# The third branch's key and value rows in a slot of the weights' ring, and score products that go out four together

## The chip, the cores and the metric

The program runs on one core of one Trainium2 chip, as one launch. The metric is the device time of that launch in microseconds (us), lower is better. The kernel before took 898.96, 900.66 and 900.21 us in three runs, median 900.21 us. One more execution, which the profiler recorded, took 896.71 us; the instructions in its trace span 895.0 us of that, and every number from a trace below is of that execution.

A core has five engines that the text names: PE (matrix products and transposes), DVE, ACT and POOL (element-wise work), SP (here it only issues transfers). Each runs its own list of instructions in order and waits on semaphores for the others. ACT, POOL and SP also issue DMA transfers; an instruction that issues one stands in the engine's list like any other and can wait there. "PEld" is the part of PE that loads the stationary operand of a product.

## What is computed

One step of a decoder layer for a prompt of 512 rows and 8 single new rows ("samples"), width 1024, all in float32:

```
mod = silu(c) @ w_ada + b_ada
h = rmsnorm(x) * (1 + scale) + shift
u, q, k_c, v_c, k_s, v_s, k_w, v_w, g = split(h @ w_in)      # 512, 512, 6 x 128, 24 columns
o_ssm  = state space mixer(u), then a GLU
o_attn = sum over 3 branches of gate * attention             # compressed, selected, window
x = x + gate1 * (concat(norm(o_ssm), norm(o_attn)) @ w_out)
x = x + gate2 * (relu(h2 @ w_up) ** 2 @ w_down)
y = rmsnorm(x)
```

There are 8 query heads and 2 key/value heads (a group of 4 query heads shares one). The prompt attends to its own rows; each sample attends to 1024 past rows of a paged cache (selected branch) or to 512 rows of a window state. Outputs are y, the new key and value rows of the three branches and the new states.

## The kernel before

**Products.** A float32 product that must be exact is made of three: the operand is split into a high part and a rest (`split`: ACT writes the high part, DVE the rest), and hi*hi, hi*lo, lo*hi go to PE. Score products whose operand is plain float32 are one `matmul` call; in the trace such a call shows as two MATMUL rows.

**Order.** The code is written in stages, and a scheduler with a timing model puts the instructions of each engine in an order of its own, interleaving the stages. So a new dependency, or a tile in another place, moves rows on all engines. Pools of tiles give the waits: a tile of a tag with `bufs=n` takes the slot of the tile n before it, and its first write waits until that one has been read.

**Weights' ring.** `rawt` hands out tiles of 128 x 2048 from a ring of three slots. Loads of weights (`wada`, `wkv`, `wq`, `wglu`) and some gathers of cache rows (`rslc`) take turns in it, each load waits until the tile three places earlier has been used. The loads are issued by SP, in SP's order.

**Key and value projection** (`kv_proj(c)`, L640, for the branches c = 0, 1, 2). It loads 256 columns of `w_in` (`wkv`), splits them into two pairs wH, wL, and runs over five row tiles t: four of 128 prompt rows and one of 8 samples. Each makes 24 products into PSUM (`pkv`; two PSUM tiles, tag `pj`). For c = 1 and 2, ACT copies the keys into `kvt` (128 x 256, tag with 2 buffers; L669), the values into `Vx`, and issues two transfers to DRAM (L691, L692); PE transposes `kvt` (`pkt`), ACT and DVE split the transposes into `KH` and `KL`. For c = 2 ACT also reads the gates. A `kvt` of t = 2 takes the buffer of t = 0, so its copy waits until the transfer of t = 0 has landed.

**State space outputs** (`state_space_outputs(q)`, q = 0 to 3). For each q eight transfers bring `yc` (one buffer), four issued by SP and four by POOL; DVE reads it into `yf` (L905, L908), and a GELU follows on ACT and DVE. The `yc` of the next q waits for `yf` of this one.

**Query projection** (L915 to L929): two `wq` loads of 1 MB, four splits, 8 x 24 products (`pj`, L619); ACT and DVE write `QS`.

**Score products in fours.** `compressed_scores` (L1170) makes for each of two key heads a set of four products (`psc`, L1174), one for each query head, each into 32 of the 128 rows of one PSUM tile. `sample_keys` (L1030) does the same for four samples: it transposes four blocks of keys each (`pkT`, L1038), copies them out of PSUM to `ktS` (the first and third on ACT, the second and fourth on DVE), and makes a set of four products (`pS`, L1047), one for each sample, again into 32 rows each. It is called for two groups of samples of the window branch (one set each) and two of the selected branch (two sets each): six sets. With the two of `psc` there are eight sets, 32 products. Each product waits for its own operand alone, and the scheduler places each where it finds it ready.

**Around them** the prompt's softmax over 16 (branch, head) pairs runs (`softmaxed`: `pst`, `mxa`, `pe`; `values`: `ptp`, `PT`, `po`). In `values` a manual dependency is there already: the first of two products waits for the copy of the second one's operand (L1272).

Of the kernel before, what the change touches and what calls it, by code (L numbers as in the profile page):

```python
# [10 lines left out]
F32 = mybir.dt.float32  # L11
# [3 lines left out]
ALU = mybir.AluOpType  # L15
AX = mybir.AxisListType

P = 128
# [19 lines left out]
def body(tc, i, o, dbg=None):  # L38
    nc = tc.nc
# [11 lines left out]
    def banks(name, **tags):  # L51

        if "pool" in bank:
            bank["pool"].close()
        st = ExitStack()
        bank.update(pool=st, tile=st.enter_context(tc.tile_pool(name=name, bufs=1, space=PS, reuse_waits="tile")), tags=tags)
# [4 lines left out]
        return bank["tile"].tile([P, 512], F32, tag=tag, name=name, bufs=bank["tags"][tag])  # L61

    banks("pA", pj=2, ss=2, tr=2, ad=1, po=1)

    def split(h, l, src):
        nc.scalar.copy(h, src)  # L66
# [4 lines left out]
    def rawt(name):  # L71
        return raw.tile([P, 2048], F32, tag="raw", name=name)
# [560 lines left out]
            nc.sync.dma_start(uscr[q * P : (q + 1) * P, T:NT], uT[q][:, T:NT])  # L633

    onames = ("cmp", "slc", "win")

    def kv_proj(c):
        c0 = 1024 + 256 * c
        r = rawt("wkv").rearrange("p (k c) -> p k c", k=KT)
        nc.sync.dma_start(r, i["w_in"][0, :, c0 : c0 + 256].rearrange("(k p) c -> p k c", p=P))  # L640
        nw = 280 if c == 2 else 256
        if c == 2:
            rg = p1.tile([P, KT, 24], F32, name="rg")
            nc.sync.dma_start(rg, i["w_in"][0, :, 1792:1816].rearrange("(k p) c -> p k c", p=P))
        ws = []
        for kk in range(2):
            kr = slice(4 * kk, 4 * kk + 4)
            h, l = whl(4, nw)
            split(h[:, :, 0:256], l[:, :, 0:256], r[:, kr])
            if c == 2:  # L650
                split(h[:, :, 256:280], l[:, :, 256:280], rg[:, kr])
            ws.append((h, l))
        for t in range(5):
            tok = slice(t * P, t * P + (P if t < 4 else NB))
            mp = P if t < 4 else NB
            ps = pst("pj", "pkv")
            for k in range(KT):
                wh, wl = ws[k // 4]
                for n, (x, w) in enumerate(((hH, wh), (hH, wl), (hL, wh))):
                    nc.tensor.matmul(ps[0:mp, 0:nw], x[:, k, tok], w[:, k % 4], start=(k == 0 and n == 0),  # L660
                                     stop=(k == KT - 1 and n == 2))
            if t == 4:
                nc.scalar.copy(kvs[:, c * 256 : (c + 1) * 256], ps[0:NB, 0:256])
                if c < 2:
                    nc.scalar.dma_start(o["new_%s_sample" % onames[c]], kvs[:, c * 256 : (c + 1) * 256])
                else:
                    nc.scalar.dma_start(o["new_win_sample"][:, T - 1], kvs[:, 512:768])
            else:
                kvt = p1.tile([P, 256], F32, tag="kvt", name="kvt", bufs=2)  # L669
                out = o["new_%s_prompt" % onames[c]][tok]  # L670
                if c == 0:
                    nc.scalar.copy(kvt, ps[:, 0:256])
                    nc.scalar.dma_start(out, kvt)
                    pk = pst("tr", "pkc")
                    for n in range(2):
                        nc.tensor.transpose(pk[:, n * P : (n + 1) * P], kvt[:, n * P : (n + 1) * P], ident)
                    for g in range(2):
                        for j2 in range(2):
                            for n in range(2):
                                nc.vector.tensor_copy(  # L680
                                    xTp[j2 * 64 : j2 * 64 + 64, n, g, :, t * 8 : t * 8 + 8],
                                    pk[g * 64 : g * 64 + 64, n * P : (n + 1) * P].rearrange(
                                        "p (c jp j2) -> p j2 jp c", c=8, j2=2)[:, j2])
                else:
                    br = c - 1

                    kv2 = kvt.rearrange("p (g a d) -> p g a d", g=2, a=2)
                    nc.scalar.copy(kv2, ps[:, 0:P].rearrange("p (g d) -> p g d", g=2).unsqueeze(2).to_broadcast([P, 2, 2, HD]))
                    vt = Vx[:, t, 2 * br : 2 * br + 2]
                    nc.scalar.copy(vt, ps[:, P:256].rearrange("p (g d) -> p g d", g=2))  # L690
                    nc.scalar.dma_start(out[:, 0:P].rearrange("t (g d) -> t g d", g=2), kv2[:, :, 0])  # L691
                    nc.scalar.dma_start(out[:, P:256].rearrange("t (g d) -> t g d", g=2), vt)  # L692
                    pk = pst("tr", "pkt")
                    for g in range(2):
                        nc.tensor.transpose(pk[:, g * P : (g + 1) * P], kvt[:, g * P : (g + 1) * P], ident)
                    split(KH[:, 2 * br : 2 * br + 2, tok], KL[:, 2 * br : 2 * br + 2, tok],
                          pk[:, 0:256].rearrange("p (g t) -> p g t", g=2))
            if c == 2:
                sigmoid_(gates[0:mp, t], ps[0:mp, 256:280])
# [215 lines left out]
    for s in range(2):  # L915
        r = rawt("wq").rearrange("p (k c) -> p k c", k=KT)
        nc.sync.dma_start(r, i["w_in"][0, :, 512 + s * 256 : 512 + (s + 1) * 256].rearrange("(k p) c -> p k c", p=P))
        for m in range(2):
            wh, wl = wsplit(r[:, :, m * P : (m + 1) * P])
            h0 = 2 * (2 * s + m)  # L920
            for hf, ps in proj_half(wh, wl):
                ql = wp.tile([P, 520], F32, tag="mrow", name="ql")[0:64].rearrange("p (a b) -> p a b", a=2)
                w = min(HB, T - hf * HB)
                for hh in range(2):
                    pq_ = ps[hh * 64 : hh * 64 + 64]
                    qc = (h0 + hh, slice(hf * HB, hf * HB + w))
                    nc.scalar.activation(ql[:, hh], pq_, AF.Copy, scale=HD**-0.5)
                    nc.scalar.activation(QS[0:64, *qc], pq_[:, 0:w], AF.Copy, scale=HD**-0.5)
                    nc.vector.tensor_tensor(QS[64:128, *qc], ql[:, hh, 0:w], QS[0:64, *qc], ALU.subtract)  # L929
            nc.gpsimd.tensor_copy(qs[:, h0 : h0 + 2], ql[:, :, HB - NB : HB])  # L930
        state_space_outputs((2 + s,))
    dump("gates", gates)
# [96 lines left out]
    def sample_keys(br, grp, tiles, nj, gate):  # L1029
# [3 lines left out]
        for h in range(nj // 4):  # L1033
            kts = []
            for b4 in range(4):
                px = pst(("ad", "ss")[b4 % 2], "pkT")
                for j4 in range(4):
                    nc.tensor.transpose(px[:, j4 * P : (j4 + 1) * P], tiles[b4][:, 4 * h + j4, 0:P], ident)  # L1038
                kt = sb.tile([P, 512], F32, tag="ktS", name="ktS", bufs=4)
                if b4 % 2:  # L1040
                    nc.vector.tensor_copy(kt, px)
                else:
                    nc.scalar.copy(kt, px)
                kts.append(kt)
            S = pst("ss", "pS")
            for b4 in range(4):
                nc.tensor.matmul(S[b4 * 32 : b4 * 32 + 32], q4[:, 4 * grp + b4], kts[b4], start=True, stop=True)  # L1047
            if br == 0:
                nc.vector.tensor_tensor(t[:, h * 512 : (h + 1) * 512].rearrange("p (j k c) -> p j k c", j=4, c=8),
                                        S.rearrange("p (j k c) -> p j k c", j=4, c=8),  # L1050
                                        pens[grp].unsqueeze(1).unsqueeze(3).to_broadcast([P, 4, 16, 8]), ALU.add)
            else:
                nc.scalar.copy(t[:, 1:nk], S[:, 1:nk])
                nc.gpsimd.memset(t[:, 0:1], NEG)
# [115 lines left out]
    def compressed_scores():  # L1170
        for g in range(2):
            ps = pst("ss", "psc")
            for hh in range(4):
                nc.tensor.matmul(ps[hh * 32 : hh * 32 + 32], Kcp[:, g], QS[:, 4 * g + hh].bitcast(F32), start=True, stop=True)  # L1174
            nc.scalar.copy(etc[:, g], ps)

    held = {}
# [72 lines left out]
    def values(br, h0, pes, po):  # L1250

        kb = 2 * br + h0 // 4
        for part in (((0, 0),), ((1, 0), (3, 3 * P)), ((2, 0),)):
# [12 lines left out]
            for kt, c0 in part:  # L1266
                for hh, PT in enumerate(PTs):
                    mm = nc.tensor.matmul(po[hh * 64 : hh * 64 + 64, kt * P : T], Vx[:, kt, kb], PT[:, c0 : c0 + T - kt * P],  # L1268
                                          start=(br == 0 and kt == 0), stop=False)
                    if hh == 0:  # L1270

                        tc.add_manual_dep(mm.ins, turned_.ins.name, mybir.DependencyInfo(mybir.DependencyClass.Sync, mybir.DependencyReason.DATA))  # L1272

    glu_w = []
    mixs = {}
# [354 lines left out]
```

## Time and profile before

| what | us |
|---|---|
| median of three runs | 900.21 |
| profiled execution, whole | 896.71 |
| profiled execution, its instructions' span | 895.0 |
| of it PE busy | 845.8 |
| DVE busy | 519.8 |
| ACT busy | 389.9 |
| from 254 on: third branch's projection, to the first query product at 273.1 | about 19 |
| 305 to 442: prompt softmax and samples' attention, PE busy 131.58 of | 137 |
| 526 to the end: MLP | 369 |

A row of the timeline has the start, the duration, the engine, the line, the operation, what it writes and reads, how many, and in brackets how long the engine sat idle before it and what ended that. "ACTq", "SPq" are rows of instructions that issue a transfer. The chain is the work that ended last, followed back from the end of the program: a piece in it is time that the end waited for. Idle time of an engine off that chain costs nothing by itself.

### The profile page before, as it was taken

What the parts mean: (1) busy time and instruction counts of PE and PEld (TensorE: products, weight loads), DVE (VectorE), ACT (ScalarE), POOL (GpSimd) and SP (SyncE); (2) the same over time, 40 slices, a digit from 0 to 9 for tenths busy, and PEclk for the clock granted to TensorE, in tenths of its full rate; (3) what the DMA queues carried; (4) which work ended last, traced back from release to release, by engine and by line L of the source; (5) the groups of instructions that cost most, each with busy time, mean ns of one, the idle gap of its engine ahead of it and who ended that gap; (6) DMA issues with size and microseconds to landing.
All of it is one profiled execution on the core that took longest, in us unless ns stands there. A gap on an engine that the chain in (4) does not pass through costs nothing.

```text
span 895.0 us, 16400 instructions
## 1 busy us (share of the span) xinstructions
PE 845.8 (94%) x6527; PEld 751.8 (84%) x6527; DVE 519.8 (58%) x1365; ACT 389.9 (44%) x883; POOL 64.0 (7%) x147
## 2 busy tenths in 40 slices
PE   2799998999998999998989999999999999999996
PEld 1557997888987766756679989999999999999996
DVE  5876666785766466668667874442333444434533
ACT  1555317453435466556655554442111344433322
POOL 6001201000152100000000000000000000000000
PEclk9999998999999999999989999999999999999998
DMA  8957577473773441203266553333333333232302
GB/s 290 319 195 247 181 157 193 138 247 116 203 244 92 165 166 64 77 2 142 73 210 198 180 190 94 94 96 94 95 95 95 94 95 92 82 86 75 92 1 96
DMA packets 111836, 122.36 MB, mean 137 GB/s; under 512 B 24500, under 2 KB 91880, under 8 KB 109584
## 3 DMA queue, kind: packets, MB, share of 16 engines
q1 hardware_dynamic: 101968, 88.66, 32.8%
q0 software_dynamic: 5488, 29.99, 9.6%
q10 hardware_dynamic: 4304, 2.66, 1.1%
q8 instruction: 51, 0.84, 0.4%
q14 instruction: 25, 0.20, 0.1%
HBM read 112.47 MB, written 13.03 MB: 140 GB/s over the span
## 4 chain that ended last, share of the span: by engine, by line
PE 66%; DVE 2%; ACT 1%; issue 0%; ACTq 0%; DVEq 0%
PE pup L1427 21%; PE pdn L1427 21%; PE pwo L1427 5%; PE pj L619 3%; PE po L1268 2%; PE ptp L1261 2%; PE pg L1289 2%; PE pS L1047 2%; PE pst L1232 1%; PE pkT L1038 1%; PE pst L1233 1%; PE psc L1174 1%; PE pstat L879 1%; PE poS L1136 0%; PE po L1349 0%; PE pst L1234 0%
## 5 line engine op out<-in xcount | busy, mean ns | idle before, releaser
L1427 PE MATMUL pdn<-hidH,wL 128*128 128x256 f32 (+1 forms) x480 | 136.0, 283 | 0.0
L1427 PE MATMUL pdn<-hidL,wH 128*128 128x256 f32 (+1 forms) x480 | 135.8, 283 | 0.0
L1427 PE MATMUL pup<-h2L,wH 128*128 128x256 f32 (+1 forms) x480 | 135.5, 283 | 0.0
L1427 PE MATMUL pdn<-hidH,wH 128*128 128x256 f32 (+1 forms) x480 | 135.3, 282 | 0.0
L1427 PE MATMUL pup<-h2H,wL 128*128 128x256 f32 (+1 forms) x480 | 135.0, 282 | 0.0
L1427 PE MATMUL pup<-h2H,wH 128*128 128x256 f32 (+1 forms) x480 | 134.5, 283 | 0.0
L1427 PEld LDWEIGHTS pup<-h2L,wH 128*128 128x128 f32 x480 | 90.4, 188 | 0.8 <-DVE rs L105 0.8
L1427 PEld LDWEIGHTS pup<-h2H,wH 128*128 128x128 f32 x480 | 89.8, 188 | 0.8 <-ACT h2H L66 0.8
L1427 PEld LDWEIGHTS pdn<-hidH,wL 128*128 128x128 f32 x480 | 90.4, 188 | 0.0
L1427 PEld LDWEIGHTS pdn<-hidL,wH 128*128 128x128 f32 x480 | 90.2, 188 | 0.1
L1427 PEld LDWEIGHTS pup<-h2H,wL 128*128 128x128 f32 x480 | 90.3, 188 | 0.0
L1427 PEld LDWEIGHTS pdn<-hidH,wH 128*128 128x128 f32 x480 | 90.3, 188 | 0.0
L66 ACT CAST wH<-wdn 128x1024 fp32r<-128x1024 f32 x30 | 31.5, 1049 | 114.2 <-PE pdn L1427 104.3
L67 DVE TENSOR_TENSOR wL<-wup,wH 128x1024 fp32r<-128x1024 f32 x30 | 36.7, 1225 | 57.9 <-ACT wH L66 57.9
L67 DVE TENSOR_TENSOR wL<-wdn,wH 128x1024 fp32r<-128x1024 f32 x30 | 36.8, 1225 | 54.3 <-ACT wH L66 54.3
L401 PE MATMUL ph<-xc,w 128*128 128x256 f32 (+2 forms) x320 | 62.9, 346 | 0.7 <-DVE xc L391 0.7
L401 PEld LDWEIGHTS ph<-xc,w 128*128 128x128 f32 x320 | 50.8, 194 | 11.0 <-issue 5.4
L66 ACT CAST wH<-wup 128x1024 fp32r<-128x1024 f32 x30 | 31.5, 1050 | 47.3 <-PE pup L1427 37.5
L1507 ACT ACTIVATE rl<-pup 128x256 f32<-128x256 f32 (+1 forms) x64 | 24.5, 385 | 45.5 <-PE pup L1427 45.4
L389 ACT COPY xc<-pxc 64x256 f32<-64x256 f32 x96 | 32.1, 366 | 22.5 <-DVE xc L391 18.8
L1508 DVE TENSOR_TENSOR rl<-rl 128x256 f32<-128x256 f32 (+1 forms) x64 | 27.2, 426 | 22.9 <-ACT rl L1507 22.9
L1436 DVE SCALAR_TENSOR_TENSOR xT<-pdn,mod,xT 128x256 f32<-128x256 f32 x32 | 15.2, 478 | 41.7 <-PE pdn L1427 41.6
(569 smaller groups left out, 2038.8 us busy)
## 6 DMA issues: line engine op xcount, KB each, us to landing
wada<-w_ada SPq DMA_DIRECT2D x20, 1024.0 KB, 5.1
wup<-w_up SPq DMA_DIRECT2D x16, 1024.0 KB, 5.4
wdn<-w_down SPq DMA_DIRECT2D x16, 1024.0 KB, 5.7
wo<-w_out SPq DMA_DIRECT2D x8, 1024.0 KB, 5.5
wada<-w_ada SPq DMA_DIRECT2D x8, 512.0 KB, 16.0
rwin<-state_win SPq DMA_DIRECT2D x4, 1024.0 KB
new_win_sample<-state_win POOLq DMA_DIRECT2D x2, 2044.0 KB, 8.6
wkv<-w_in SPq DMA_DIRECT2D x3, 1024.0 KB, 8.1
```

Of the source, the lines that this page charges most:

```text
L66: nc.scalar.copy(h, src)
L67: nc.vector.tensor_tensor(l, src, h, ALU.subtract)
L389: nc.scalar.copy(dst[:, :, :, hf], srcv[:, :, :, hf])
L401: nc.tensor.matmul(phv[:, lo:hi, 0:w], w1[n][:, r_], xc[n][:, lo:hi, r_ % 8, off : off + w], start=(r_ == 0), stop=(r_ == 15))
L619: nc.tensor.matmul(ps[:, 0:HB], w[:, k], x[:, k, hc], start=(k == 0 and n == 0), stop=(k == KT - 1 and n == 2))
L1047: nc.tensor.matmul(S[b4 * 32 : b4 * 32 + 32], q4[:, 4 * grp + b4], kts[b4], start=True, stop=True)
L1261: nc.tensor.transpose(pt_[:, c : c + P], at(qt, kt * P, P), ident)
L1268: mm = nc.tensor.matmul(po[hh * 64 : hh * 64 + 64, kt * P : T], Vx[:, kt, kb], PT[:, c0 : c0 + T - kt * P], start=(br == 0 and kt == 0), s ...
L1289: nc.tensor.matmul(ps[:, 0:HB], r[:, k, c], zf[k][:, hc], start=(k == 0), stop=(k == 3))
L1427: nc.tensor.matmul(ps[:, 0 : b - a], w, x[:, a:b], start=first and n == 0, stop=last and n == 2)
L1507: nc.scalar.activation(rl, ps[:, 0 : b - a], AF.Relu)
L1508: nc.vector.tensor_tensor(rl, rl, rl, ALU.mult)
```

## The change

Three things. First, for c = 2 one tile of the weights' ring is taken behind `wkv` (`kvr`), and the keys of row tile t go to columns t*256 to t*256+255 of it, instead of to the two buffers of the tag `kvt`. Second, in `sample_keys` the first product of a set gets a dependency on the copies of the third and the fourth operand; third, in `compressed_scores` the first product of a set gets one on the last write of the fourth head's `QS`. The helper `not_before` makes such a dependency; `values` uses it in place of the same lines.

```diff
+    def not_before(mm, last):
+        tc.add_manual_dep(mm.ins, last.ins.name, mybir.DependencyInfo(mybir.DependencyClass.Sync, mybir.DependencyReason.DATA))
...
+    qlast = {}
...
+        kvr = rawt("kvt") if c == 2 else None
         for t in range(5):
...
-                kvt = p1.tile([P, 256], F32, tag="kvt", name="kvt", bufs=2)
+                kvt = kvr[:, t * 256 : (t + 1) * 256] if c == 2 else p1.tile([P, 256], F32, tag="kvt", name="kvt", bufs=2)
...
-                    nc.vector.tensor_tensor(QS[64:128, *qc], ql[:, hh, 0:w], QS[0:64, *qc], ALU.subtract)
+                    qlast[h0 + hh] = nc.vector.tensor_tensor(QS[64:128, *qc], ql[:, hh, 0:w], QS[0:64, *qc], ALU.subtract)
...
-                if b4 % 2:
-                    nc.vector.tensor_copy(kt, px)
-                else:
-                    nc.scalar.copy(kt, px)
-                kts.append(kt)
+                kts.append((kt, (nc.scalar.copy, nc.vector.tensor_copy)[b4 % 2](kt, px)))
             S = pst("ss", "pS")
             for b4 in range(4):
-                nc.tensor.matmul(S[b4 * 32 : b4 * 32 + 32], q4[:, 4 * grp + b4], kts[b4], start=True, stop=True)
+                mm = nc.tensor.matmul(S[b4 * 32 : b4 * 32 + 32], q4[:, 4 * grp + b4], kts[b4][0], start=True, stop=True)
+                if b4 == 0:
+                    not_before(mm, kts[2][1])
+                    not_before(mm, kts[3][1])
...
-                nc.tensor.matmul(ps[hh * 32 : hh * 32 + 32], Kcp[:, g], QS[:, 4 * g + hh].bitcast(F32), start=True, stop=True)
+                mm = nc.tensor.matmul(ps[hh * 32 : hh * 32 + 32], Kcp[:, g], QS[:, 4 * g + hh].bitcast(F32), start=True, stop=True)
+                if hh == 0:
+                    not_before(mm, qlast[4 * g + 3])
```

No instruction is added or removed on any engine; the scheduler moves rows between the end of branch 1's projection and the end of the attention. Three places matter below. In the rows, a name has its tile's number behind it, and the brackets list the semaphores of a wait by engine or, for transfers, by number (DMAHW for transfers of SP and ACT, DMASW for those of POOL). Line numbers behind the helper are larger in the changed kernel: L1047 is L1050 there, L660 is L667, L903 is L910, L917 is L924.

**PE, the second set of the selected branch's first group** (`pS` from `ktS`; `po` and `ptp` belong to the prompt's softmax). Before:

```order
L1056 MATMUL psn_4253<-knT_3386,q4_3377 128x8 [waits Activation_49]
L1047 MATMUL pS_4247<-ktS_4224,q4_3377 32x512 [waits DVE_49]
L1047 MATMUL pS_4247<-ktS_4231,q4_3377 32x512
L1047 MATMUL pS_4247<-ktS_4238,q4_3377 32x512
L1268 MATMUL po_4379<-PT_4451,Vx_2577 64x512 [waits Activation_49]
L1268 MATMUL po_4379<-PT_4458,Vx_2577 64x512
L1261 MATMUL ptp_4469<-ident_66,pe_4416 128x128 [waits PE_49]
L1261 MATMUL ptp_4469<-ident_66,pe_4416 128x128
L1261 MATMUL ptp_4469<-ident_66,pe3_4415 128x128 x2
L1047 MATMUL pS_4247<-ktS_4245,q4_3377 32x512 [waits DVE_49]
```

and now:

```order
L1270 MATMUL ptp_4450<-ident_66,pe_4413 128x128 [waits DVE_49] x2
L1270 MATMUL ptp_4450<-ident_66,pe3_4412 128x128 [waits DVE_49]
L1063 MATMUL psn_4250<-knT_3383,q4_3374 128x8 [waits Activation_49]
L1050 MATMUL pS_4244<-ktS_4221,q4_3374 32x512 [waits DVE_49]
L1050 MATMUL pS_4244<-ktS_4228,q4_3374 32x512
L1050 MATMUL pS_4244<-ktS_4235,q4_3374 32x512
L1050 MATMUL pS_4244<-ktS_4242,q4_3374 32x512
L1277 MATMUL po_4376<-PT_4448,Vx_2577 64x512 [waits Activation_49]
```

The fourth product stood behind other work and now stands with the three; in the changed kernel all eight sets are four rows in a row, where before the two sets of `psc` lay in six pieces and the six sets of `pS` in thirteen.

**SP, the loads of wq** (`yc` in fours for each q, `wq` the query weights, `rwin` window state, `wglu` the GLU's weights). Before:

```order
L640 DMA wkv<-w_in 128x8x256 x2
L785 DMA mscr<-M_2385 128x64
L835 DMA yscr<-ys 128x320
L917 DMA wq<-w_in 128x8x256 x2
L787 DMA Tz<-mscr 128x8x64
L785 DMA mscr<-M_2487 128x64
L903 DMA yc<-yscr 16x8x80 x4
L787 DMA Tz<-mscr 128x8x64
L903 DMA yc<-yscr 16x8x80 x2
L835 DMA yscr<-ys 128x320
L903 DMA yc<-yscr 16x8x80 x5
```

and now:

```order
L792 DMA mscr<-M_2487 128x64
L910 DMA yc<-yscr 16x8x80 x8
L794 DMA Tz<-mscr 128x8x64
L842 DMA yscr<-ys 128x320
L910 DMA yc<-yscr 16x8x80 x4
L842 DMA yscr<-ys 128x320
L910 DMA yc<-yscr 16x8x80
L924 DMA wq<-w_in 128x8x256 x2
L910 DMA yc<-yscr 16x8x80 x3
L1172 DMA rwin<-state_win 128x2x1024 x3
L1287 DMA wglu<-ssm_w_glu 128x4x512
```

The two loads of `wq` moved behind thirteen of the sixteen `yc` transfers, the last of which (q = 3) waits until DVE has read the `yc` of q = 2; the ring's extra tile makes each load wait for one tile later.

**ACT, row tiles 1 to 3 of the third branch** (`kvt`, `Vx`, `gates` out of PSUM, the two transfers, `KH`). Before, from the transfer of t = 1's values:

```order
L692 DMA new_win_prompt<-Vx_2577 128x128 [waits DMAHW5_49,Activation_49]
L66 CAST KH_2575<-pkt_2860 128x2x128 [waits PE_49]
L688 COPY kvt_2892<-pkv_2867 128x256 [waits DMAHW1_49,PE_49]
L690 COPY Vx_2577<-pkv_2867 128x128
L117 ACTIVATE gates_104<-pkv_2867 128x24
L691 DMA new_win_prompt<-kvt_2892 128x2x64 [waits DMAHW0_49,Activation_49]
L692 DMA new_win_prompt<-Vx_2577 128x128 [waits Activation_49]
L688 COPY kvt_2929<-pkv_2904 128x256 [waits DMAHW3_49,PE_49]
```

and now:

```order
L699 DMA new_win_prompt<-Vx_2577 128x128 [waits DMAHW7_49,Activation_49]
L695 COPY kvt_2793<-pkv_2866 128x256 [waits PE_49]
L697 COPY Vx_2577<-pkv_2866 128x128
L121 ACTIVATE gates_104<-pkv_2866 128x24
L70 CAST KH_2575<-pkt_2859 128x2x128 [waits PE_49]
L698 DMA new_win_prompt<-kvt_2793 128x2x64 [waits DMAHW0_49,Activation_49]
L699 DMA new_win_prompt<-Vx_2577 128x128 [waits DMAHW1_49,Activation_49]
L70 CAST KH_2575<-pkt_2895 128x2x128 [waits PE_49]
L695 COPY kvt_2793<-pkv_2902 128x256 [waits PE_49]
```

The copies into `kvt` no longer wait for a transfer. The transfers that ACT issues wait for the semaphore that they reuse; DMAHW7 and DMAHW0 are, in the changed kernel, the numbers on which the first reads of the two `wq` loads wait.

More of the change, by code (lines that the diff above doesn't have):

```diff
@@ L1270, in values @@
                     if hh == 0:
-                        tc.add_manual_dep(mm.ins, turned_.ins.name, mybir.DependencyInfo(mybir.DependencyClass.Sync, mybir.DependencyReason.DATA))
+                        not_before(mm, turned_)
     glu_w = []
```

## The prediction

> **What bounds the kernel now.** I read the busy times first, then the chain of work that ended last, then windows over the attention.
>
> ```profile
> PE 845.8 (94%) x6527; PEld 751.8 (84%) x6527; DVE 519.8 (58%) x1365; ACT 389.9 (44%) x883; POOL 64.0 (7%) x147
> ...
> PE 66%; DVE 2%; ACT 1%; issue 0%; ACTq 0%; DVEq 0%
> PE pup L1427 21%; PE pdn L1427 21%; PE pwo L1427 5%; PE pj L619 3%; PE po L1268 2%; PE ptp L1261 2%; PE pg L1289 2%; PE pS L1047 2%; PE pst L1232 1%; PE pkT L1038 1%; PE pst L1233 1%; PE psc L1174 1%; PE pstat L879 1%; PE poS L1136 0%; PE po L1349 0%; PE pst L1234 0%
> ```
>
> PE is busy for 94% of the span, and nearly every piece of the chain is PE's. The score products stand in it by name: `pS` with 2%, `psc` with 1%. So PE time saved there is worth itself, as long as PE stays the limit. The windows (length; then busy time with count of PE, PEld, DVE, ACT, POOL; granted clock; DMA share; GB/s) show how far that holds:
>
> ```profile
> 305.00:442.00 137.00, 131.58 (x990) 89.10 (x990) 94.81 (x296) 85.64 (x238) 7.08 (x12) 1.00 0.25 91
> 400.00:416.00 16.00, 13.17 (x151) 11.24 (x150) 13.16 (x37) 10.97 (x32) 1.93 (x2) 1.00 0.53 198
> ```
>
> From 305 to 442 PE idles for 5.4 us of 137, while DVE is busy for 69%: PE is the limit. In the 16 us from 400 on both are busy for 13.2 us, so there DVE is no less a limit, and that piece cannot shrink by PE's savings alone.
>
> **The products.** By groups, and then in the chain (start, length, engine, tile, rows; a product is two MATMUL rows):
>
> ```profile
> L1047 PE MATMUL pS<-ktS,q 128*32 128x512 f32 x48 | 14.4, 605 | 0.0
> L1174 PE MATMUL psc<-QS,Kcp 128*32 128x512 f32 x16 | 6.3, 604 | 0.0
> ```
>
> ```profile
> 287.40 0.98 PE psc L1174 x4
> ...
> 294.35 0.98 PE psc L1174 x4
> ...
> 298.41 0.97 PE psc L1174 x2
> ...
> 307.23 0.98 PE psc L1174 x2
> ...
> 312.03 1.72 PE pS L1047 x6
> 314.47 0.97 PE pS L1047 x2
> ...
> 393.30 0.99 PE pS L1047 x6
> ...
> 429.93 0.98 PE pS L1047 x2
> ```
>
> A piece of one product (x2) costs 0.98 us, one of two (x4) 0.98, and one of three (x6, at 393.30) 0.99. Products that write different 32 rows run beside each other when nothing stands between, and one that is alone pays the whole 0.98. `psc` lies in six pieces (287.40 to 307.23; the last four hold one product each): 6 x 0.98 = 5.9 us. `pS` lies in thirteen (312.03 to 429.93): twelve of 0.98, and one at 312.03 of 1.72 with a gap inside, 13.5 us. The change makes two pieces and six. A piece of four does not occur in these two groups; I bound it by 0.98 below (as three) and by two pieces above, and take 0.98, the row of three being the nearest. Four column groups at once are there in another product:
>
> ```profile
> 306.80 0.43 PE pkT L1038 x4
> ...
> 320.77 1.01 PE poS L1136 x32
> ```
>
> Four transposes over the whole array take 0.43 us, 0.11 each; 32 rows of `poS`, each into a quarter of the array, take 1.01, 0.03 each. So I count psc 5.9 - 2 x 0.98 = 3.9 us and pS 13.5 - 6 x 0.98 = 7.6 us saved: **-11.5 us**.
>
> The Trainium skill ("TensorE: Matmul & The Clock Gate", section "Part 3: Packing small matmuls — row/col tiling") states measured gains of 2.38 for three column tiles and 3.07 for four row tiles, against 3 and 4 in full. By the second a set of four would take 4 x 0.98 / 3.07 = 1.28 us and eight sets would save 2.4 us less, an estimate by that page. By the first a piece of three would take 1.23; the row at 393.30 has 0.99, so the measurement decides.
>
> **The wait that each set now has.** Before, a product went out when its own operand was copied; now the first waits for all four, and behind it in PE's list wait the other three and whatever follows: transposes, `pst` and `po` of the prompt's softmax. Idle time that ended before `pS` rows (us, times; two of five rows), the copy out of PSUM, and the softmax work that stands ahead of copies on DVE:
>
> ```profile
>   issue: 1.2, 7
> ...
>   ACT ktS L1043: 0.6, 1
> ```
>
> ```profile
> L1041 DVE COPY ktS<-pkT 128x512 f32<-128x512 f32 x12 | 8.1, 679 | 1.1 <-PE pkT L1038 1.1
> ...
> L1238 DVE TENSOR_REDUCE mxa<-pst 128x1 f32<-128x512 f32 x16 | 11.0, 687 | 1.9 <-PE pst L1234 1.8
> ...
> L1238 DVE TENSOR_REDUCE mxa<-pst 128x1 f32<-128x128 f32 x16 | 4.6, 285 | 4.2 <-PE pst L1234 4.1
> ...
> L1247 DVE TENSOR_SCALAR pe<-pe,dn 128x512 f32<-128x512 f32 x16 | 7.7, 479 | 0.0
> ...
> L1247 DVE TENSOR_SCALAR pe<-pe,dn 128x128 f32<-128x128 f32 x16 | 4.5, 284 | 0.4
> ```
>
> The two `psc` sets should wait for nothing: the fourth head's `QS` is old by the time the scheduler sends them. A `pS` set costs at least -0.2 (the 1.2 us of issue gaps gone with the loose pieces, over six sets) and at most 1.37 (its last copy, 0.68, behind the longest reduction, 0.69, with PE empty meanwhile). The one time that a set does wait for a copy is in the rows, 0.6 us; I take that for each: **+3.6 us** for six (from -1.2 to +8.2).
>
> **The third branch's rows.** The row tiles' copies into `kvt`, and a later transpose of them:
>
> ```profile
> 266.68 0.37 ACT L688 COPY kvt<-pkv 128x256 f32<-128x256 f32 x1 [2.87 <-DMA new_win_prompt<-kvt]
> ...
> 270.67 0.37 ACT L688 COPY kvt<-pkv 128x256 f32<-128x256 f32 x1 [3.35 <-DMA new_win_prompt<-kvt]
> ```
>
> ```profile
> 264.00:270.00 6.00, 5.66 (x45) 4.58 (x44) 1.71 (x4) 0.64 (x3) 0.70 (x2) 1.00 1.02 384
> 270.00:274.00 4.00, 1.56 (x9) 0.67 (x7) 1.74 (x5) 2.88 (x8) 1.41 (x3) 1.00 0.59 134
> 274.00:278.00 4.00, 3.82 (x19) 3.80 (x20) 3.85 (x8) 1.78 (x4) 0.91 (x1) 0.57 0.02 6
> ```
>
> ACT waits 2.87 and 3.35 us until a transfer has landed, in a stretch where all DMA engines are full (share 1.02). PE has nothing left to do, since the two `pkv` tiles are read by these copies: 0.34 + 2.44 + 0.18 = 3.0 us idle in the three windows. Then its clock is granted at 0.57 for 4 us, which costs 4 x 0.43 = 1.7 us. The most to be had here is 4.7 us. The Trainium skill (same page, section "Part 1: The HAM clock gate (the \"warmup\" mystery)") states half clock after an idle window of about 3.4 us; the 0.57 right behind a window that is 39% busy agrees, and by that rule a shorter gap would bring the 1.7 us too.
>
> The ring slot removes ACT's wait, but the slot and the new order delay the `wq` loads. These stand on SP behind `yc` of q = 3, which waits for DVE's `yf` of q = 2, and that now stands behind the splits of `wkv` and the GELU of q = 1:
>
> ```profile
> 250.88 1.07 DVE L905 SCALAR_TENSOR_TENSOR yf<-uT,vec,yc 128x512 f32<-128x512 f32 x1
> ...
> 256.74 0.70 DVE L127 TENSOR_TENSOR uT<-zt,yf 128x520 f32<-128x520 f32 x1
> ```
>
> ```profile
> 226.93 1.76 SPq L917 DMA_DIRECT2D wq<-w_in  x2
> ```
>
> ```profile
> 238.97 0.37 ACT L66 CAST KH<-pkt 128x256 fp32r<-128x256 f32 x1 [3.59 <-DMA wq<-w_in]
> ```
>
> ```profile
> wkv<-w_in SPq DMA_DIRECT2D x3, 1024.0 KB, 8.1
> ```
>
> The GELU's last row ends at 257.4, so `wq` is issued at about 257.8 (up to 258.5 if that `yf`, 1.07 us by its row, lies behind), the second load 0.9 us later (1.76 / 2). A load of this size lands after 8.1 us (`wkv`); the second `wq` itself took about 10 (227.8 to the end of ACT's wait behind it). It lands at 258.7 + 8.1 = 266.8, at most 258.5 + 0.9 + 10 = 269.4. ACT's transfer of the keys of t = 2 reuses the semaphore of that load and now waits for it, and behind it in ACT's list stand the next transfer and a `KH` (about 0.85 + 0.37), then the last row tile's copy: 268.1 in place of 270.67. What follows that copy is as before. **-2.6 us**, with ends of -4.7 (all of it) and 0 (the load at 269.4). `rwin` and `wglu`, the transfers that filled the DMA engines before, go out later; they are needed from 306 on, so the attention has them in time.
>
> **Sum.** -11.5 + 3.6 - 2.6 = -10.5 us on the profiled execution's 896.71 us: 886.2. That execution is 3.5 us under the median of the runs, 900.21 (they lie within 1.7 us), so the same difference gives **889.7 us**. The best of these ends is -11.5 - 1.2 - 4.7 = -17.4, 882.8; the worst is -11.5 + 8.2 + 0 = -3.3, 896.9.
>
> **Rivals.**
> *The weights come late.* For: the wait on the `wq` semaphore is real in the order, and 10 us have been seen. Against: DMA is freer without `rwin` ahead. No gain or up to 3 us lost (the load in the place of ACT's old 2.87 wait): -7.9 to -4.9, 892.3 to 895.3, middle 893.8.
> *The path moves to the softmax.* For: the window from 400, where DVE and ACT carry 13.2 and 11.0 us of 16; PE freed there only waits for them. Against: PE idles for only 4% of the whole attention. A third of 11.5 would stay, and the new waits fall into idle time: 3.8 less, 896.4.
> *Slower: sets held behind softmax rows.* The last copy stands on DVE behind a whole pair's reductions, 4 x (0.687 + 0.285) / 2 = 1.9 us, with half the time its divisions too, 4 x (0.479 + 0.284) / 2 = 1.5, and its own 0.68: 3.4 us a set, while PE's list is blocked. Six sets cost 20.2 us against 14.1 saved: +6.1, 906.3. It decides from 14.1 / 6 = 2.4 us a set. For: PE cannot pass a waiting row, and DVE is busy for 69% here. Against: the scheduler knows of the dependency and puts other rows ahead of the set; the one wait seen is 0.6 us.
> *The change doesn't do what it says.* A fourth product does not run beside three: eight sets take 0.98 more each, 7.8 us, and -2.7 is left: 897.5. For: no piece of four in the rows. Against: `poS` with four quarters.
>
> **How the numbers follow.** Chances: forecast 0.58, late weights 0.16, softmax 0.13, held sets 0.09, no fourth product 0.04. The range goes from the best end to the rivals at 897.5, with 0.9 us for the runs' spread below: 882 to 897.5; outside lie the held sets and the edges of the others. A measurement of this kernel tells 0.2%, 1.8 us, from no change: 898.4 to 902.0 is "same". Late weights with long waits, or the softmax keeping everything, end there: 0.08. Slower 0.09, faster 0.83.
>
> **What would show it.** In the changed profile: eight pieces of `psc` and `pS` of x8 at about 0.98 in the chain (two times 0.98 each would be the fourth rival); idle before `pS` by `ktS` of about 0.6 a set (over 2.4: the slower rival); ACT's `kvt` copies with no DMA before them, a transfer of `new_win_prompt` that waits for `wq` instead, the query products' stream starting at about 272 in place of 274.7, and a granted clock above 0.57 behind it; the window from 305 shorter by 7 us or more (less, with DVE as busy as PE: the softmax). An order on chip that leaves PE idle elsewhere, which no row of before shows, would make all of it wrong.

## The result, and the profile after

| kernel | us, median | runs | ratio to before, 95% interval |
|---|---|---|---|
| before, same comparison | 899.59 | 4 | |
| changed | 884.67 (884.02 to 885.30) | 4 | 0.9834 (0.9817 to 0.9851) |
| changed, second comparison (before 899.14) | 886.57 | 4 | 0.9851 (0.9825 to 0.9878) |

The change is worth 14.9 us in the first comparison and 12.6 in the second (by the medians; by the ratio 13.4). The profiled executions differ by 12.3 us (896.71 and 884.39): that of before lies 2.9 us under its median, that of the changed kernel 0.3 under its own. So a part of the 14.9 is not in the two traces; the part on the prediction says where it may lie.

The busy times and the chain's shares of the changed kernel, as shown of before:

```profile
span 882.7 us, 16408 instructions
...
PE 834.7 (95%) x6527; PEld 750.6 (85%) x6527; DVE 521.1 (59%) x1365; ACT 389.6 (44%) x883; POOL 64.0 (7%) x147
...
PE 64%; DVE 2%; ACT 1%; DMA 1%; issue 0%; ACTq 0%; DVEq 0%
```

PE is busy for 11.1 us less, with the same 6527 instructions, and the span is 12.3 shorter. The other engines have their old busy times to within 1.3 us. In the traces the gain is nearly all PE time. The score products in the chain (start, length, tile, rows):

```profile
290.12 0.99 PE psc L1181 x8
...
300.17 1.00 PE psc L1181 x8
...
332.26 0.99 PE pS L1050 x8
...
383.14 0.99 PE pS L1050 x8
```

Every piece is a whole set of four (x8, two rows a product), and takes 0.99 or 1.00 us (1.06 for one more, at 409.46), where one product alone took 0.98. Four of the six `pS` sets stand among the chain's long pieces; the other two are no longer on it.

What was taken back can be seen in the same attention stretch, from the last query product to the samples' last `poS`, with the part behind it up to the MLP. First before, then changed (length; PE, PEld, DVE, ACT, POOL busy; granted clock; DMA share; GB/s):

```profile
302.20:441.70 139.50, 134.08 (x1002) 90.58 (x1000) 96.84 (x303) 88.08 (x243) 8.82 (x22) 1.00 0.25 91
441.70:506.00 64.30, 60.46 (x459) 55.84 (x452) 47.91 (x122) 36.35 (x65) 0.96 (x1) 0.95 0.62 201
```

```profile
296.90:430.80 133.90, 125.97 (x999) 90.06 (x997) 96.75 (x305) 87.03 (x242) 9.08 (x22) 0.99 0.27 95
430.80:493.70 62.90, 59.80 (x463) 55.28 (x456) 47.24 (x119) 36.83 (x66) 0.96 (x1) 0.97 0.63 205
...
402.00:406.00 4.00, 4.00 (x20) 3.81 (x21) 1.66 (x5) 2.59 (x6) 0.00 (x0) 0.57 0.23 96
```

In both stretches together PE works 8.8 us less (194.54 to 185.77), but it idles 1.8 us more (9.26 to 11.03), and from 402 to 406 it now works at a granted clock of 0.57, 4 x 0.43 = 1.7 us. Two places of the changed kernel's chain show whom PE waits for:

```profile
303.14 0.69 DVE mxa L1247
...
307.62 1.18 DVE pe L1256 x4
...
311.87 0.21 DVE pe L1256
...
393.87 7.99 DMA rslc<-cache_slc,pidx
```

From 303.1 to 312.1 the end waits for DVE alone, for softmax work and copies of `ktS`; before, PE products stood in the chain there. At 393.87 an 8 us gather of cache rows stands in it, behind which lies the stretch at half clock.

Laid out from fixed points in the two traces, the 12.3 us are: +1.2 up to the first product of `kv_proj` (116.5 and 117.7), -2.8 from there to the first query product with the low part (158.2 and 155.4), -3.8 for the query products (27.5 and 23.7), -5.6 for the attention, -1.3 for the part behind it. The MLP takes 389.0 us in both, counted from its first product (506.0 and 493.7); the table of before counts from 526, inside it.

### The profile page after: what moved, and what is told of

It is laid out like the page before. It is cut to its first block, busy times and chain, and to the rows that moved or that the text cites. A ratio compares the mean times of both kernels' runs of the same rounds, so it can differ in the third digit from the quotient of the medians.

```text
span 882.7 us, 16408 instructions
## 1 busy us (share of the span) xinstructions
PE 834.7 (95%) x6527; PEld 750.6 (85%) x6527; DVE 521.1 (59%) x1365; ACT 389.6 (44%) x883; POOL 64.0 (7%) x147
## 4 chain that ended last, share of the span: by engine, by line
PE 64%; DVE 2%; ACT 1%; DMA 1%; issue 0%; ACTq 0%; DVEq 0%
PE pup L1435 21%; PE pdn L1435 21%; PE pwo L1435 5%; PE pj L623 3%; PE po L1277 2%; PE ptp L1270 2%; PE pg L1297 2%; PE pkT L1045 1%; PE pst L1241 1%; DMA rslc<-cache_slc,pidx 1%; PE pst L1242 1%; PE poS L1143 1%; DVE mxa L1247 1%; PE pstat L886 1%; PE pS L1050 0%; DVE pe L1256 0%
## 5 line engine op out<-in xcount | busy, mean ns | idle before, releaser
L405 PE MATMUL ph<-xc,w 128*128 128x256 f32 (+2 forms) x320 | 64.9, 354 | 0.7 <-DVE xc L395 0.7
L405 PEld LDWEIGHTS ph<-xc,w 128*128 128x128 f32 x320 | 52.7, 202 | 11.2 <-issue 5.6
L1251 ACT ACTIVATE pe<-pst,mxa 128x512 f32<-128x512 f32 (+1 forms) x64 | 33.7, 536 | 15.3 <-DVE mxa L1247 12.9
## 6 DMA issues: line engine op xcount, KB each, us to landing
wada<-w_ada SPq DMA_DIRECT2D x8, 512.0 KB, 14.9
```

Source lines behind the costliest of these rows:

```text
L405: nc.tensor.matmul(phv[:, lo:hi, 0:w], w1[n][:, r_], xc[n][:, lo:hi, r_ % 8, off : off + w], start=(r_ == 0), stop=(r_ == 15))
L1251: nc.scalar.activation(at(qt, 0, nk), d, AF.Exp, bias=mx[:, qt : qt + 1], accum_out=dn[:, qt : qt + 1])
```

## The experiments

Two questions were open: what each part of the change gives, and by which mechanism. Each table line below is a kernel against the kernel before; the us are (ratio - 1) x 899.

**The parts one by one.** The first six kernels leave out parts of the change.

`e1_scores_only`: the two score dependencies, with `kvt` as before.

```diff
-        kvr = rawt("kvt") if c == 2 else None
-                kvt = kvr[:, t * 256 : (t + 1) * 256] if c == 2 else p1.tile([P, 256], F32, tag="kvt", name="kvt", bufs=2)
+                kvt = p1.tile([P, 256], F32, tag="kvt", name="kvt", bufs=2)
```

> The two score dependencies alone, the third branch's rows in two kvt buffers as before (wq loads keep their place on SP). If the products running beside each other pay (13 + 6 pieces become 8, 0.98 us each, 11.5 us less) and the waits that the changed trace shows before pS (1.9 us in all) are all that comes back: -9.6 us, 890.0, ratio 0.989. If a set's waits cost 0.6 us each as forecast: -7.9, ratio 0.991. Rival, PE waits for DVE and ACT instead in the attention and gets back less than half: -5 or less, ratio 0.9945 or more. Second rival, the whole change is worth more than its parts: then this and the rows alone together give clearly less than 14.9.

`e2_rows_only`: the rows in the ring's tile, without both score dependencies.

```diff
-                if b4 == 0:
-                    not_before(mm, kts[2][1])
-                    not_before(mm, kts[3][1])
...
-                if hh == 0:
-                    not_before(mm, qlast[4 * g + 3])
```

> The rows of the third branch in the ring's tile alone, no new score dependency; pS lies in 14 pieces in this order (13 before), psc in 6. If the rows give what the two traces show up to the query stream and in its clock (1.6 us of start, 1.2 us of another start of the run, 1.7 us of clock, 4.5 in all), less 1.0 for the piece: -3.5 us, ratio 0.996, stream of query products at a granted clock of 1.00. By the forecast's own term, -2.6 without the clock, less 1.0: -1.6, ratio 0.998. Rival, the late wq loads cost what the copies gain: 0, ratio 1.000.

`e3_psc_only` and `e4_ps_only`: `kvt` as before (the edit of e1), and the first three of these lines taken out, or the last two.

> The dependency in compressed_scores alone. psc in 2 pieces instead of 6 (-3.9 us), but in this order pS lies in 15 pieces instead of 13 (+2.0): -1.9 us, ratio 0.998. If the order apart from the pieces decides, it can be anywhere within 4 us of that, on either side.

> The dependency in sample_keys alone. pS in 6 pieces instead of 13 (-7.6 us), psc in 6 as before; waits of 0.3 us a set as in the changed trace: -5.7 us, ratio 0.9937; of 0.6 us a set as forecast: -4.0, ratio 0.9955. Rival, the saved PE time turns into waits for DVE and ACT: -2 or less, ratio 0.998 or more.

`e5_rows_ps` and `e6_rows_psc`: the changed kernel with the last two of them taken out, or the first three.

> The changed kernel without the dependency in compressed_scores: rows in the ring and pS in sets of four, psc in six pieces as before. If the parts add up (rows -4.9, pS -8.3 as measured alone): -13.2 us, ratio 0.985. If the psc dependency costs 3 us as it did alone, this is faster than the changed kernel, -14.9 - 3 = -18, ratio 0.980; if its two sets save the pieces' 3.9 us inside the whole change, it is slower, -11, ratio 0.988.

> Rows in the ring and the dependency in compressed_scores, none in sample_keys (pS in 15 pieces). If the parts add up: -4.9 + 3.0 = -1.9 us, ratio 0.998. If the 3 us of psc alone came from one order that happened to have the gathers late, they go away here and the pieces' -1.9 stands: -6.8, ratio 0.9925.

| rows in ring | psc | pS | kernel | ratio, 95% interval | us |
|---|---|---|---|---|---|
| no | yes | yes | e1 | 0.9895 (0.9876 to 0.9914) | -9.4 |
| yes | no | no | e2 | 0.9945 (0.9927 to 0.9964) | -4.9 |
| no | yes | no | e3 | 1.0033 (1.0018 to 1.0047) | +3.0 |
| no | no | yes | e4 | 0.9907 (0.9890 to 0.9924) | -8.4 |
| yes | no | yes | e5 | 0.9858 (0.9837 to 0.9879) | -12.8 |
| yes | yes | no | e6 | 0.9982 (0.9969 to 0.9995) | -1.6 |
| yes | yes | yes | changed | 0.9834 (0.9817 to 0.9851) | -14.9 |

The rows and the scores add up: -4.9 and -9.4 make -14.3, the whole is -14.9. So do the rows and `pS` (-13.3 by adding, -12.8 in e5). `pS` alone gave more than expected (-8.4 against -5.7); in e4's trace the part behind the attention is 4.3 us shorter than before, at a granted clock of 1.00 where before has 0.95:

```profile
438.30:498.30 60.00, 56.43 (x449) 52.27 (x442) 45.93 (x115) 35.78 (x64) 0.96 (x1) 1.00 0.65 215
```

The clocks of the runs point the same way. Span x (1 - mean granted clock) is an estimate, from the span and clock of each run, of what half clock costs it. In the mean it is 14.7 us before, 10.2 in e4 and 13.8 in e1. So about 4.5 of e4's 8.4 us are clock.

The `psc` part does not stand alone: without `pS` it makes the kernel slower, twice (e3 to before, and e6 to e2, +3.3 us); with `pS` it is worth -1.0 (e1 to e4) and -2.2 (changed to e5), both with intervals that overlap. By the same estimate `psc` beside `pS` takes off about 4.4 us without the clock (e1 against e4), near the 3.9 of its pieces, and loses 3.6 to it; why the clock differs between these orders was not tested. In e3 `pS` lies in its 15 pieces and covers 15.4 us of PE time (13.5 before); that is in the expectation of -1.9 already, and 5 us more have to be found. They are in the attention stretch of e3, in its waits of PE for ACT, and in its chain:

```profile
304.00:450.60 146.60, 138.23 (x1004) 92.61 (x1006) 97.80 (x308) 88.29 (x243) 9.17 (x22) 0.99 0.25 87
```

```profile
PE pst L1236 <- ACT pe L1246: 4.4, 4, 1.7
```

```profile
414.83 11.08 DMA rslc<-cache_slc,pidx x2
```

The stretch is 7.1 us longer than before, PE idles 8.4 us in it instead of 5.4 and is busy for 4.1 more, of which 1.7 come from half clock between 320.4 and 323.8; the softmax wait is 4.4 us (2.3 before), and 11 us of gathers stand in the chain. Since e6 shows the same (147.3 us, idle 8.8), it comes with this order and not with one run. Why the scheduler's order for `psc` in fours without `pS` in fours has these waits stays open.

**Is it the products beside each other, or only a new order?** `e7_serial_ps` keeps all dependencies and sets, and takes away that the four of a set write different rows (it leaves out the right scores of the samples).

```diff
-                mm = nc.tensor.matmul(S[b4 * 32 : b4 * 32 + 32], q4[:, 4 * grp + b4], kts[b4][0], start=True, stop=True)
+                if b4 == 0:
+                    mm = nc.tensor.matmul(S, q4[:, 4 * grp : 4 * grp + 4].rearrange("p b x -> p (b x)"), kts[b4][0], start=True, stop=True)
+                else:
+                    mm = nc.tensor.matmul(S[0:32], q4[:, 4 * grp + b4], kts[b4][0], start=True, stop=True)
```

> The changed kernel, but in each pS set the first product is one of 128 columns that writes all rows, and the other three all write rows 0 to 31, so that the four cannot run beside each other (the scores of the other samples are then not computed rightly). Same sets of four, same dependencies. If the gain is that the four run beside each other: each of three products adds two passes of 0.43 us, 2.6 us a set, six sets 15.6: -14.9 + 15.6 = +0.7 us against before, ratio 1.001. Rival, the new order is what gained: at most 4 us come back, -11, ratio 0.988.

Measured: 0.9956 (0.9936 to 0.9976), -4.0 us against before, 11.0 slower than the changed kernel (the expectation had 15.6). A set in its chain, the full product and the other three:

```profile
340.58 0.86 PE pS L1051 x2
341.43 2.69 PE pS L1053 x6
```

A set takes 0.86 + 2.69 = 3.55 us of PE instead of 0.99, 2.56 more; six sets make 15.4, as expected. Over a quarter of it does not reach the end: PE idles 3.0 us less from the query products to the MLP than in the changed kernel (8.0 and 11.0), since waits that PE had there are now filled. It also runs at full clock there, where the changed kernel has two stretches at half clock that cost it 1.7 us each. What each of the two accounts for was not parted. Running beside each other is most of the gain.

**What do the rows gain by?** The prediction had the copies freed of a wait for a transfer. A rival came up with the trace: the moved `wq` loads push `rwin` and `wglu`, 4 MB, out of the time in which these transfers run. `e8_ring_hold` moves the loads and keeps the waits.

```diff
+        kvr = rawt("kvt") if c == 2 else None
+        if c == 2:
+            nc.gpsimd.memset(kvr[:, 0:1], 0.0)
...
                 nc.scalar.copy(kvs[:, c * 256 : (c + 1) * 256], ps[0:NB, 0:256])
+                if c == 2:
+                    nc.scalar.copy(kvr[0:NB, 0:1], kvs[:, 512:513])
```

> No score dependency; kvt stays in two buffers, but a ring tile is taken behind wkv and held until the samples' rows (one small memset and one small copy write it), so the second wq load, rwin and wglu go out later as with the rows in the ring, while the copies into kvt still wait for the transfers. pS lies in 11 pieces (13 before): -2.0 us. If the rows' gain is that the copies no longer wait: query stream as far behind the projection as before (158 us from the first product of the first branch), clock of 0.57 behind the gap, -2.0 us, ratio 0.998. Rival, the gain is that rwin and wglu no longer fill the DMA engines ahead of the small transfers: the stream starts 2 to 3 us earlier at full clock, -5 to -7 us, ratio 0.994 to 0.992.

Measured: 0.9986 (0.9968 to 1.0004). The total agrees with the first theory, the trace with the rival. A copy still waits for a transfer, but PE does not:

```profile
267.77 0.37 ACT L699 COPY kvt<-pkv 128x256 f32<-128x256 f32 x1 [2.85 <-DMA new_win_prompt<-kvt]
```

```profile
270.00:274.00 4.00, 4.00 (x31) 2.85 (x30) 1.84 (x5) 2.62 (x8) 0.00 (x0) 1.00 1.02 397
```

Up to the end of the query products it is 3.9 us faster than before (181.8 us from the first `kv_proj` product, 185.7 before), and it gives 3.6 back between there and the MLP. With the second `wq` load late and the first early it is not a clean test, so the next kernel holds back `rwin` and `wglu` alone. (The last `yc` transfers, which stood behind these loads on SP from 270.67 on, thereby go out by 267.2.) `e9_hold_only` (`lastw[0]` is the last transfer of the third branch's values):

```diff
-            nc.sync.dma_start(r, i["state_win"][0, b : b + 2].rearrange("b (c j) a g d -> c b (j a g d)", j=4))
+            rw = nc.sync.dma_start(r, i["state_win"][0, b : b + 2].rearrange("b (c j) a g d -> c b (j a g d)", j=4))
+            not_before(rw, lastw[0])
...
-        nc.sync.dma_start(r, i["ssm_w_glu"][0].rearrange("(k p) c -> p k c", p=P))
+        gw = nc.sync.dma_start(r, i["ssm_w_glu"][0].rearrange("(k p) c -> p k c", p=P))
+        not_before(gw, lastw[0])
```

> The kernel before with one change: the loads of rwin and wglu get a dependency on the last transfer of the third branch's rows (t = 3), so they no longer fill the DMA engines beside these transfers. kvt keeps its two buffers and its waits, the ring has no extra tile, the wq loads keep their early place, no score dependency (pS in 14 pieces, 13 before: +1.0 us). If the rows' gain comes from the crowded DMA: the copies into kvt wait for less than 1 us, the query stream starts 3 to 4 us earlier at full clock (1.5 us more), -4 us, ratio 0.9955. If it comes from the copies having no transfer to wait for, only the private columns do it: +1.0, ratio 1.001.

> The two score dependencies as in the changed kernel, with the loads of rwin and wglu held back as in the run before instead of the rows in the ring. If crowding is the cause, this is the scores alone (-9.5 us, ratio 0.9895) and the rows' 4.9 with it: -14.4, ratio 0.984, the same as the changed kernel; the wq loads stay early, and no ACT transfer waits for them. If the private columns are needed: -9.5, ratio 0.9895.

Measured: e9 0.9951 (0.9931 to 0.9970), -4.4 us; e10, the same with the two score dependencies, 0.9834 (0.9812 to 0.9856), -14.9. Both come out as crowding has it. The transfers of the third branch's rows, issue to landing (minimum, median, maximum), before and then in e9, with a copy into `kvt` of e9 behind them:

```profile
DMA to landing us min/median/max: 2.4/5.4/8.4
```

```profile
DMA to landing us min/median/max: 1.7/1.7/1.7
```

```profile
269.52 0.37 ACT L695 COPY kvt<-pkv 128x256 f32<-128x256 f32 x1 [1.06 <-PE pkv L667]
```

With two buffers, as before, the copies wait for their products and no longer for transfers, because a transfer of 64 KB now lands in 1.7 us. The Trainium skill ("DMA: Bandwidth & Descriptors", section "Issuing engines are not separate DMA queues") says that transfers issued by different engines run on the same 16 engines and interleave; ACT's small transfers beside SP's loads agree (5.4 us in the median with them, 1.7 without). The private columns of the ring are not needed for the gain. e10 and the changed kernel in the same comparison (0.9851, 0.9825 to 0.9878) cannot be told apart.

**What else holds the query products?** `e11_pool_rows` issues the eight transfers from POOL, `e12_changed_again` is the changed kernel beside it.

```diff
-                    nc.scalar.dma_start(out[:, 0:P].rearrange("t (g d) -> t g d", g=2), kv2[:, :, 0])
-                    nc.scalar.dma_start(out[:, P:256].rearrange("t (g d) -> t g d", g=2), vt)
+                    eng = nc.gpsimd if c == 2 else nc.scalar
+                    eng.dma_start(out[:, 0:P].rearrange("t (g d) -> t g d", g=2), kv2[:, :, 0])
+                    eng.dma_start(out[:, P:256].rearrange("t (g d) -> t g d", g=2), vt)
```

> The changed kernel with the third branch's eight row transfers issued by POOL instead of ACT, so that no copy stands behind a transfer that waits for a wq load. If that wait (2.5 to 3.5 us on ACT, twice) still holds the query stream: it starts up to 1.5 us earlier (PE idles 1.45 us from 264 to 274 in the changed trace), -16.4 us against before, ratio 0.982. Rival, the stream is held by the landing of wq and its split, not by ACT's transfers: no change, -14.9, ratio 0.9834.

> The changed kernel as it is, beside the three others on the same chip, so that they can be compared directly: -14.9 us against before as measured first, ratio 0.9834 (0.9817 to 0.9851). If a good part of that came from a slow sample of the kernel before: nearer to the profiles' difference, -12.3, ratio 0.986.

Measured: e11 0.9860 (0.9835 to 0.9885), e12 0.9851: no gain, and neither expectation named the reason. The edit moved more than the issuer. SP issues `rwin` at 262.35 (268.11 in the changed kernel), but `yc` of q = 3 lands no later for it: its transfers take up to 9.5 us from issue to landing, 9.6 in the changed kernel. What takes longer is `yf`. First e11, then the changed kernel:

```profile
271.40 1.75 DVE L913 SCALAR_TENSOR_TENSOR yf<-uT,vec,yc 128x512 f32<-128x512 f32 x1 [1.53 <-DMA yc<-yscr]
273.08 0.78 DVE L916 SCALAR_TENSOR_TENSOR yf<-uT,vec,yc 128x8 f32<-128x8 f32 x1
```

```profile
270.28 1.08 DVE L912 SCALAR_TENSOR_TENSOR yf<-uT,vec,yc 128x512 f32<-128x512 f32 x1
271.28 0.22 DVE L915 SCALAR_TENSOR_TENSOR yf<-uT,vec,yc 128x8 f32<-128x8 f32 x1
```

The windows of both, and the first PE row behind e11's gap:

```profile
270.00:274.00 4.00, 2.23 (x18) 1.56 (x16) 2.60 (x3) 1.16 (x2) 3.99 (x7) 1.00 1.02 384
274.00:278.00 4.00, 2.90 (x13) 2.88 (x14) 4.00 (x6) 2.45 (x6) 2.96 (x4) 0.56 1.00 404
```

```profile
270.00:274.00 4.00, 2.55 (x17) 1.91 (x16) 3.57 (x8) 3.13 (x6) 0.00 (x0) 1.00 0.98 381
```

```profile
275.10 0.27 PE L1012 MATMUL pkn<-ident,kvs 8*128 8x8 f32 x1 [2.87 <-ACT kvs L670]
```

The same two rows take 1.1 and 0.2 us for every other q of the two kernels. In e11 POOL works beside them for 3.99 of the four microseconds from 270, in the changed kernel not at all, since its element-wise rows there now come between and behind its transfers. The low part of `wq` on DVE and the copy `kvs` on ACT both come behind this `yf`; PE waits 2.87 us, and its clock halves. That POOL's work is what slows DVE fits these rows and was not tested apart.

## Why the prediction came out as it did

The forecast was 889.7 us within 882.0 to 897.5; measured were 884.67 and 886.57, faster as forecast, by more than the forecast's 10.5 us.

- **Products, forecast -11.5 us: right.** By the length of their pieces, `pS` went from 13.5 to 6.1 us and `psc` from six pieces of 0.98 to two of 0.99: -11.3. The step that no row of before showed, a fourth product beside three, stands in the x8 rows at 0.99. The Trainium skill ("TensorE: Matmul & The Clock Gate", section "Part 3: Packing small matmuls — row/col tiling") has 3.07 as the gain of four row tiles; here four column tiles take 0.99 where one takes 0.98, which is 4 x 0.98 / 0.99 = 3.96. Against e7's set, whose products do not run beside each other, the gain is 3.55 / 0.99 = 3.6.
- **Waits, forecast +3.6 us: the place wrong, and the size right by luck.** Idle time before `pS` in the changed kernel (us, times):

```profile
  DVE ktS L1047: 1.0, 2
  issue: 0.7, 3
```

Two of the six sets wait for a copy, 1.0 us in all, not 0.6 each. What comes back is elsewhere, 1.8 us of more idle time and 1.7 at half clock, about DVE's stretch from 303 to 312 and the gather at 394; that these make about 3.6 is luck. That is a mild form of the rival "the path moves to the softmax", at another place than the window from 400 that it named. So the attention is 5.6 us shorter, where the prediction looked for 7 or more.
- **Rows, forecast -2.6 us: too small, and the cause not the one named.** Alone they gave -4.9 (0.9927 to 0.9964). In the traces the query products begin 2.8 us earlier, as forecast, and by the path that was forecast: the last row tile's copy starts at 269.21, which is 268.0 without the later start of 1.2 us (forecast 268.1). The granted clock behind the gap is 1.00 instead of 0.57 (the row below), and the products take 1.5 us less for that, which the forecast named as an end and left out of the sum. The step that failed is the one that gives the gain to the ring slot. The prediction noted that `rwin` and `wglu` go out later, asked only whether they come in time, and put their move at nothing; e9 shows that this move gives the gain without the slot. What the slot adds beside the move is small: from the first `kv_proj` product to the last query product, e8 (loads moved, no slot) takes 181.8 us and e2 (loads moved, slot) 180.3, before 185.7, and e8 is at half clock for 6.8 us more than e2 on that way. The late `wq` did what the prediction said of it: issued at 257.23 (forecast 257.8), and ACT's copies stand behind transfers that wait for it.

```profile
257.23 1.19 SPq L924 DMA_DIRECT2D wq<-w_in  x2
```

```profile
264.52 0.37 ACT L695 COPY kvt<-pkv 128x256 f32<-128x256 f32 x1 [2.46 <-DMA wq<-w_in]
```

```profile
274.00:278.00 4.00, 4.00 (x36) 4.00 (x35) 2.92 (x9) 1.84 (x5) 1.05 (x1) 1.00 1.04 408
```

- **Rivals.** Late weights: the wait on `wq` came and cost PE little. It idles 1.28 us before its first query product, whose operand ACT casts behind these waits; from the first `kv_proj` product to the last query product the changed kernel takes 179.1 us, and e10, with `wq` early, 178.6. Held sets: did not come; yet e3 shows that a dependency of this kind can make the kernel slower, by an order with more waits and not by the wait itself. No fourth product: refuted.
- **The rest is in the clock.** The terms as measured (-11.3, -2.8, -1.5, +1.8 and +1.7) make -12.1. At the start, where nothing was changed, the changed kernel lost 1.2 us; its trace has a stretch at half clock there that before has not. Behind the attention, before is at half clock for 6.83 us and the changed kernel for 3.41, which is worth 1.7 us. First before, then changed:

```profile
458.91:465.74 6.83, 6.29 (x27) 6.04 (x28) 5.25 (x16) 3.87 (x11) 0.00 (x0) 0.50 0.23 73
```

```profile
40.39:43.81 3.42, 3.42 (x14) 2.63 (x12) 0.72 (x2) 0.26 (x1) 0.00 (x0) 0.50 1.05 387
...
449.99:453.41 3.42, 3.42 (x16) 3.36 (x17) 3.26 (x9) 1.65 (x5) 0.00 (x0) 0.50 0.02 5
```

With +1.2 and -1.7 the terms make -12.6 of the profiles' -12.3. Over the whole span both profiled executions have a mean clock of 0.987, so the clock gives nothing to their difference. It does to the medians: the runs of before that stand beside e5 to e8 have clocks of 0.981 to 0.987, 0.983 in the mean, and the changed kernel's in the first comparison 0.987 or 0.988. By the estimate used for e4 that is about 3.8 us, more than the 2.6 by which the first comparison exceeds the profiles; in the second comparison (0.984 and 0.985 in the mean) it is 0.7. Whether the change itself brings the higher clock was not tested.

## What to carry to other kernels

A product that fills a quarter of the array cost as much alone (0.98 us) as with three neighbours (0.99), so where a chain shows many pieces of equal length with different row counts, count the pieces, not the rows; a wait for the last operand is cheap where other work can be put ahead of it. When an edit moves loads, ask of each load that is moved what it was crowding, not only who waits for it. Test parts together as well as alone: one part of this change is a loss without its neighbour.

## What had not been expected of the hardware

The granted clock fell without one long gap. Before, PE's longest idle time from 264 to 278 was 1.33 us, but in the four microseconds from 270 it was busy for only 1.56 us, and the clock behind was 0.57. In the changed kernel the longest was 1.28 us, it was busy for 2.55 us of these four, and the clock stayed at 1.00. So an idle gap of the length of the half-clock stretch (3.41 us) is not needed. The Trainium skill ("TensorE: Matmul & The Clock Gate", section "HAM oscillation — how this bites in real kernels") speaks of idle gaps over about 3.4 us; no gap of that length is in these rows, so they do not bear out the prediction's word that the 0.57 agrees with such a rule. The busy share of PE alone does not decide either. Elsewhere in the trace of before the clock stayed at 1.00 behind a window with 1.76 us of 3.41 busy (52%), and halved (the row from 458.91 above) behind one with 2.19 (64%):

```profile
407.72:411.13 3.41, 1.76 (x14) 1.48 (x14) 3.37 (x9) 2.13 (x7) 0.70 (x1) 1.00 1.06 373
411.13:414.54 3.41, 2.29 (x17) 1.84 (x16) 3.41 (x7) 2.91 (x9) 0.00 (x0) 1.00 1.01 420
455.50:458.91 3.41, 2.19 (x19) 1.89 (x17) 1.75 (x13) 2.85 (x5) 0.00 (x0) 1.00 1.10 348
```

What decides stays open.

And transfers of 64 KB took between 2.4 and 8.4 us beside 4 MB of loads, and 1.7 us each without them.
